# Output projection of a hybrid decoder layer in seven block products instead of eight, on one Trainium2 core

## The chip, the core and the metric

The kernel runs on one core of a Trainium2 chip. The metric is the time of one execution in device microseconds. TensorE (PE in the profile) multiplies, with its weight loads (PEld) beside it; VectorE (DVE) and ScalarE (ACT) work on tiles; GpSimd (POOL) does some element work and issues the accumulating DMAs; SyncE (SP) issues most DMAs.

## The reference

One decoder layer on 1024 tokens of width 1024. A normalised input goes through one in-projection to three groups of heads: four HGRN2 heads, a windowed attention mixture, and RWKV-7. Their outputs, side by side, are the rows that the output projection multiplies:

```
h <- h + W_out [ HGRN2(A) | dilated-window attention mixture(B) | RWKV-7(C) ](W_in rmsnorm(h))
h <- h + gated MLP with causal depthwise conv (width 3) on rmsnorm(h)
h <- h + sigmoid(rmsnorm(h) W_g) * (p[layer] W_p)
```

followed by a final RMSNorm. W_out is 1024 by 1024, so the output projection is a 1024 by 1024 by 1024 product. Everything is float32.

## The kernel before

Tokens lie along the free dimension, features over 128 partitions: a matrix of 1024 features is eight tiles of 128 by 1024, and most work is on token halves of 512 (HT). A float32 product is made of three TensorE products. Each factor is split into a rounded high part and the rest, and the sum takes high by high, high by low and low by high (`mm3`, the three matmul lines L142, L144, L146). A weight block of 128 output features is loaded by one DMA of 512 KB on SP (`load_w`, L105, two buffers `wraw`). `split2` makes its high part `whi` by a cast on ACT (L114) and its low part `wlo` either by a subtraction on DVE or POOL (L120), or by a negation on ACT (L117) and an accumulating DMA on GpSimd that adds the weights from DRAM to it (L118). There are six `whi` and six `wlo` buffers of half a block each.

The stages run in this order: norm of the input; in-projection, RWKV-7 (`rwkv`, head pairs 6 and 7), HGRN2 and window attention (tiles 0 to 3 and 4, 5), with the in-projection blocks of later heads fed between the steps of a head as filler for TensorE (`project_rest`); output projection (`phase_out`); the MLP, whose products are already made by a seven-product scheme (`mul`, L1343 and L1644); per-layer embedding; final norm.

Within an engine instructions run in the order in which they stand in its queue. A scheduler sets that order when the kernel is built, from a cost estimate of each instruction; `issue_after(x)` in the code holds back what is created under it until x stands in the order. The queues themselves are in order at run time, so an instruction that waits holds all behind it on its engine, and a waiting DMA issue on SP holds all later transfers of that queue.

Around RWKV-7, ACT makes `lora`, `sg` and `kksq` (squares of the keys), TensorE sums them (`kks`, L563), ACT makes the decay `w` (L573, L577), DVE its running product and inverse, ACT and DVE `r` (L506, L507), and TensorE the scores `sc` (L659). SP carries `sc` through DRAM (`scz`, `At`, L669, L675) to a DVE recurrence (`Tt`, `Tb`, L683, L685). At the end of the last HGRN2 head DVE updates the states `hst` (L1078), TensorE makes `hpo`, ACT and DVE normalise `ho` (L1091 to L1102), and TensorE transposes it (`vt`, L1108).

The output projection takes the eight head tiles as operands. `o_split` splits each as soon as its head is done, the low part of one token half on DVE, of the other on POOL. `phase_out` loads h (eight DMAs on ACT's queue), takes weight blocks in 14 turns (blocks 0 and 1 for both token halves, the others once for each half, so each is loaded twice), adds each product to h and stores it. The squares of the first half go to a sum (`sq_acc`), from which TensorE makes the norm factor (`ps_ss`, L188) while the second half is still being multiplied. It makes 8 blocks x 8 head tiles x 2 halves x 3 parts = 384 matmuls of 128x128 by 128x512.

## Time and profile before

| | |
|---|---|
| median of 3 runs | 1402.65 us (1402.52 to 1405.57) |
| the profiled execution | 1403.29 us, of which 1401.5 us are the span of its instructions |
| granted TensorE clock | 0.996 of full speed over the span |
| PE busy | 1373.6 us, 98% |
| DVE, ACT, POOL busy | 1042.6, 644.2, 361.7 us |
| the output phase | from 557 us (its first products, beside the last head) to 643 us (first product of the embedding) |

A row of the timeline reads: start, duration, engine, line, operation, out<-in, shapes, count, and in brackets the idle time before it and what ended that. In grouped rows the count is followed by busy time, mean ns of one, and idle time ahead of the group.

### The profile page before, as it was taken

The page shows a single profiled execution, that of the slowest core. Times are in us where ns is not written, and L with a number is a line of the kernel's source. Part 1 is how long each engine was busy: PE and PEld are TensorE (multiplying, and loading weights), DVE is VectorE, ACT ScalarE, POOL GpSimd, SP SyncE. Part 2 cuts the span into 40 slices and gives each one's busy share as a digit, 9 for nine tenths or more (in the row PEclk, how much of TensorE's full clock was granted, in tenths as well). Part 3 has the DMA queues.
Part 4 walks back from the last instruction along what each step waited for, and adds up shares of the span by engine and source line. Part 5 has one row for each costly group of instructions (what it writes and reads, how often), then busy time and mean ns, then how long its engine had stood idle before and what let it go on. Part 6 is the DMA issues. An engine that isn't in the chain of part 4 may idle for free.

```text
span 1401.5 us, 22421 instructions
## 1 busy us (share of the span) xinstructions
PE 1373.6 (98%) x8646; PEld 1114.8 (80%) x8646; DVE 1042.6 (74%) x1614; ACT 644.2 (46%) x1107; POOL 361.7 (26%) x286
## 2 busy tenths in 40 slices
PE   9999999999999999999999999999999999999997
PEld 6878777877878767788788888888888888888886
DVE  7595456835667795458889888888888799778675
ACT  7523323133355584365544343444344444455662
POOL 4210011101222232111345455445453000002231
PEclk9999999999999999999999999999999999999998
DMA  6344322533723322873232322232324963442674
GB/s 231 90 119 101 91 69 68 133 72 88 244 91 106 99 69 89 267 224 130 97 128 98 113 102 88 101 109 98 113 98 163 354 211 113 120 150 62 174 196 149
DMA packets 88475, 182.83 MB, mean 130 GB/s; under 512 B 20912, under 2 KB 23216, under 8 KB 88368
## 3 DMA queue, kind: packets, MB, share of 16 engines
q1 hardware_dynamic: 66784, 147.05, 31.0%
q0 software_dynamic: 9360, 18.88, 7.3%
q10 hardware_dynamic: 12224, 15.47, 3.2%
q8 instruction: 68, 1.11, 0.3%
q14 instruction: 39, 0.32, 0.1%
HBM read 134.96 MB, written 46.40 MB: 129 GB/s over the span
## 4 chain that ended last, share of the span: by engine, by line
PE 83%; issue 7%; DVE 5%; ACT 2%; POOL 2%; DMA 1%; SPq 0%; POOLq 0%; DVEq 0%; ACTq 0%
PE bg L1343 17%; PE bv L1343 13%; PE bv L1644 7%; PE bg L1644 7%; PE dp L142 6%; PE dp L146 6%; PE dp L144 6%; PE swq L1174 1%; PE bv L142 1%; PE bv L146 1%; PE bv L144 1%; PE hsc L1020 1%; PE zp L142 1%; PE bg L142 1%; PE bg L146 1%
## 5 line engine op out<-in xcount | busy, mean ns | idle before, releaser
L142 PE MATMUL dp<-xh,whi 128*128 128x512 f32 x544 | 187.1, 406 | 2.5 <-ACT xh L413 1.2
L144 PE MATMUL dp<-xl,whi 128*128 128x512 f32 x544 | 180.3, 393 | 0.6 <-DVE xl L414 0.5
L146 PE MATMUL dp<-xh,wlo 128*128 128x512 f32 x544 | 179.6, 392 | 0.5 <-DMA wlo<-in_w_out_dram 0.5
L120 POOL TENSOR_TENSOR wlo<-raw,whi 128x512 fp32r<-128x512 f32 x84 | 134.8, 1623 | 75.7 <-ACT whi L114 75.7
L114 ACT CAST whi<-wraw 128x512 fp32r<-128x512 f32 x120 | 72.9, 617 | 153.5 <-PE dp L144 115.4
L1343 PE MATMUL bg<-t,whi 128*128 128x512 f32 x352 | 133.4, 389 | 0.0
L144 PEld LDWEIGHTS dp<-xl,whi 128*128 128x128 f32 x544 | 102.3, 188 | 24.7 <-DVE xl L414 2.6
L146 PEld LDWEIGHTS dp<-xh,wlo 128*128 128x128 f32 x544 | 102.1, 188 | 24.7 <-issue 2.0
L142 PEld LDWEIGHTS dp<-xh,whi 128*128 128x128 f32 x544 | 98.9, 189 | 27.3 <-issue 5.9
L120 POOL TENSOR_TENSOR wlo<-s,whi 128x512 fp32r<-128x512 f32 x44 | 64.6, 1467 | 166.9 <-ACT whi L114 153.7
L1644 PE MATMUL bg<-t,whi 128*128 128x512 f32 x308 | 95.2, 390 | 0.0
L114 ACT CAST whi<-raw 128x512 fp32r<-128x512 f32 x88 | 52.5, 619 | 92.7 <-issue 48.6
L1644 PE MATMUL bv<-t,whi 128*128 128x512 f32 x308 | 94.8, 389 | 0.0
L114 ACT CAST whi<-s 128x512 fp32r<-128x512 f32 x66 | 38.9, 620 | 119.5 <-PE bg L1343 112.8
L1343 PEld LDWEIGHTS bg<-t,whi 128*128 128x128 f32 x352 | 66.0, 188 | 13.7
L118 POOL DMA_DIRECT2D wlo<-in_w_in_dram x28 | 24.8, 898 | 190.0 <-ACT wlo L117 161.6
L195 POOL TENSOR_TENSOR rst<-rst,mhalf 128x4 f32<-128x4 f32 (+1 forms) x9 | 10.1, 1127 | 233.7 <-DVE rst L191 218.0
L1640 ACT CAST t<-t 128x512 fp32r<-128x512 f32 x77 | 47.8, 622 | 45.4 <-PE bv L1644 31.1
L1343 PE MATMUL bg<-t,wlo 128*128 128x512 f32 x176 | 67.5, 389 | 0.0
L1644 PEld LDWEIGHTS bv<-t,whi 128*128 128x128 f32 x308 | 57.8, 188 | 12.0
L1644 PEld LDWEIGHTS bg<-t,whi 128*128 128x128 f32 x308 | 57.8, 188 | 11.9
L120 DVE TENSOR_TENSOR wlo<-wraw,whi 128x512 fp32r<-128x512 f32 x60 | 44.8, 751 | 29.4 <-ACT whi L114 16.5
(423 smaller groups left out, 3464.8 us busy)
## 6 DMA issues: line engine op xcount, KB each, us to landing
raw<-in_ffn_up_dram SPq DMA_DIRECT2D x44, 512.0 KB, 3.3
wraw<-in_w_in_dram SPq DMA_DIRECT2D x28, 512.0 KB, 3.8
z<-zst SPq DMA_DIRECT2D x18, 512.0 KB, 3.2
gb<-ct SPq DMA_DIRECT2D x33, 256.0 KB, 2.1
t<-gb SPq DMA_DIRECT2D x33, 256.0 KB, 2.8
t<-gt SPq DMA_DIRECT2D x33, 256.0 KB, 2.7
zl<-z SPq DMA_DIRECT2D x16, 512.0 KB, 4.6
wraw<-in_ple_gate_dram SPq DMA_DIRECT2D x16, 512.0 KB, 3.8
```

The source lines that it names most:

```text
L114: self.cast = nc.scalar.copy(hi, src).ins
L118: nc.gpsimd.dma_start(lo, eng, accum_op=ALU.add)
L120: eng.tensor_tensor(lo, src, hi.bitcast(F32), ALU.subtract)
L142: nc.tensor.matmul(ps[hf], wh, xh[hf], start=first, stop=False)
L144: nc.tensor.matmul(ps[hf], wh, xl[hf], start=False, stop=False)
L146: self.step = nc.tensor.matmul(ps[hf], wl, xh[hf], start=False, stop=last).ins
L195: nc.gpsimd.tensor_tensor(r2, r, self.mhalf[:, :n], ALU.pow)
L1020: nc.tensor.matmul(sc[g:g + 64, c, :], ks[:, c * P + g:c * P + g + 64], x, start=True, stop=True)
L1174: m = nc.tensor.matmul(pq[h][:, b:b + w], d["q"][hs, qb * P:nk], d["k"][hs, b:b + w], start=True, stop=True)
L1343: nc.tensor.matmul(ps, w[part == 2][:, s], X[k][part == 1], start=start and k == part == 0, stop=k == 3 and part == 2, skip_group_check=no ...
L1640: nc.scalar.copy(xh, x)
L1644: nc.tensor.matmul(ps[m], wt[part == 2][:, m * P:(m + 1) * P], (xh, xl)[part == 1], start=k == part == 0, stop=k == NK - 1 and part == 2)
```

## The change

The output projection is written as a 2 by 2 block product: W_out in four quarters (rows and columns of 512), the operand in four quarters (four heads by one token half each). Seven products of quarter size replace the eight. Each is four row blocks of 12 matmuls (four 128-rows by three parts), so 28 jobs and 336 matmuls.

- The products take sums and differences of quarters. Those of the operand are made by `o_done` and in `phase_out`: differences on DVE, negations on ACT, and eight accumulating DMAs on GpSimd within SBUF. Each sum is split into high and low by `pair`, always cast on ACT and subtracted on DVE (before, half of the 16 subtractions were POOL's).
- Four of the seven products take sums of quarters of W_out. `out_sums` makes these early, in steps that `project_rest` takes twice per in-projection block from the RWKV-7 stage on. For each of four row blocks it makes two loads of 256 KB on SP, three negations on ACT, five accumulating DMAs on GpSimd and four stores to DRAM on SP: 8 loads, 12 negations, 20 accumulating DMAs and 16 stores in all. Their two tiles have the buffers that `sq_acc` uses (`sqt`).
- All 28 jobs are held in one fixed order by `issue_after(self.ends[-1])`. Weights are loaded as 256 KB halves, five jobs ahead. The low parts of the first 10 are made on DVE, those of the other 18 by ACT and an accumulating DMA (before, 14 by the latter).
- The rows of W_out are put into the order of the heads on the host; the operand buffers of the first token half are two pools instead of one; the embedding's loads share the weights' two `wraw` buffers instead of two of their own.

The core of the diff:

```diff
+    def out_sums(self):
+        nc, wo = self.nc, self.a["w_out"]
+        self.S = [{n: self.zpool.tile([P, HT], F32, tag=f"ws{n}{i}", name=f"ws{n}{i}") for n in "1234"} for i in range(4)]
+        for i in range(4):
+            a11, a12, a21, a22 = (wo[m][:, c] for m in (i, 4 + i) for c in (slice(0, HT), slice(HT, T)))
+            t, u = (self.spool.tile([P, HT], F32, tag="sqt", name=self.nm("wsum"), bufs=2) for _ in (0, 1))
+            def turn(x):
+                nc.scalar.activation(x, x, AF.Copy, scale=-1.0)
+            def add(x, src):
+                nc.gpsimd.dma_start(x, src, accum_op=ALU.add)
+            nc.sync.dma_start(t, a21)
+            nc.sync.dma_start(u, a22)
+            yield
+            turn(t)
+            add(u, a21)
+            yield
+            nc.sync.dma_start(self.S[i]["1"], u)
+            add(t, a11)
+            yield
+            nc.sync.dma_start(self.S[i]["3"], t)
+            turn(u)
+            yield
+            turn(t)
+            add(u, a11)
+            yield
+            add(t, a22)
+            add(u, a12)
+            yield
+            nc.sync.dma_start(self.S[i]["2"], t)
+            nc.sync.dma_start(self.S[i]["4"], u)
+            yield
...
     def project_rest(self, js):
+                if k in (1, 5):
+                    next(self.sums, None)
...
+    FIRST, LAST = (6, 7, 0, 1), (4, 2, 3, 5)
+    def pair(self, dst, src, eng=None):
+        nc = self.nc
+        hi, lo = dst
+        nc.scalar.copy(hi, src)
+        (eng or nc.vector).tensor_tensor(lo, src, hi.bitcast(F32), ALU.subtract)
+    def o_done(self, k):
...
+        o = [self.o[k][:, HT:], self.o[k][:, :HT]]
+        if k in self.FIRST:
+            i = self.FIRST.index(k)
+            t1, t3 = self.Eo[i]
+            nc.vector.tensor_tensor(t1, o[1], o[0], ALU.subtract)
+            self.pair(self.A[i], o[0])
+            self.pair(self.B[i], t1)
+            nc.scalar.activation(t1, t1, AF.Copy, scale=-1.0)
+            nc.scalar.activation(t3, o[1], AF.Copy, scale=-1.0)
+            return
...
+        for t in self.Eo[i][::-1]:
+            nc.gpsimd.dma_start(t, self.parts[k, 1], accum_op=ALU.add)
     def phase_out(self, hp, x0, emb):
...
+        plan = {"p1": (A, "a", 0, 1), "p5": (B, "b", 4, 0), "p3": (D, "b", 0, 0), "p6": (A, "a", 0, 0),
+                "p7": (B, "a", 4, 0), "p2": (C, "c", 0, 1), "p4": (A, "a", 4, 1)}
+        jobs = [(n, i) for n in plan for i in range(4)]
...
+            with ExitStack() as order:
+                if self.ends:
+                    order.enter_context(self.tc.issue_after(self.ends[-1]))
+                self.mul((ps, ws.pop((n, i)), X, start))
+            self.ends.append(self.step)
...
+        for n, (p, i) in enumerate(jobs):
+            for q in range(0 if n == 0 else n + 4, min(n + 5, len(jobs))):
+                ws[jobs[q]] = weight(*jobs[q])
+            job(p, i)
+            for go in extra.get(n, ()):
+                go()
```

Where instructions move, at three places. First ACT in the RWKV-7 preparation. Before, from the first in-projection copy after the norm factor:

```order
L506 ACTIVATE lora_452<-raw_449,omm 128x1024
L502 COPY raw_456<-dp_160 128x1024
L114 CAST whi_654<-wraw_647 128x512
L506 ACTIVATE k_467<-dp_161,omm 128x1024
L514 ACTIVATE lora_452<-lora_452 64x1024
L506 ACTIVATE sg_459<-raw_456,omm 128x1024
L560 ACTIVATE kksq_477<-k_467,par 128x1024
L114 CAST whi_846<-wraw_844 128x512
```

and in the changed kernel, where `wsum` are the tiles of `out_sums`:

```order
L546 ACTIVATE lora_455<-raw_452,omm 128x1024
L542 COPY raw_459<-dp_163 128x1024
L114 CAST whi_677<-wraw_670 128x512
L546 ACTIVATE k_470<-dp_164,omm 128x1024
L554 ACTIVATE lora_455<-lora_455 64x1024
L440 ACTIVATE wsum_1118<-wsum_1118 128x512
L546 ACTIVATE sg_462<-raw_459,omm 128x1024
L600 ACTIVATE kksq_480<-k_470,par 128x1024
L114 CAST whi_873<-wraw_871 128x512
```

The first negation of the second row block's tile now stands between `lora` and `sg`.

Second SP's queue over the same stretch and after it. Before:

```order
L105 DMA wraw_518<-in_w_in_dram 128x1024
L105 DMA wraw_611<-in_w_in_dram 128x1024
L105 DMA wraw_647<-in_w_in_dram 128x1024
L105 DMA wraw_844<-in_w_in_dram 128x1024
L105 DMA wraw_920<-in_w_in_dram 128x1024
```

and in the changed kernel (`wsum_654`, `wsum_655` are the two tiles of the first row block, `wsum_1118`, `wsum_1119` of the second, `ws` the sums in DRAM):

```order
L105 DMA wraw_614<-in_w_in_dram 128x1024
L446 DMA wsum_655<-in_w_out_dram 128x512
L105 DMA wraw_670<-in_w_in_dram 128x1024
L451 DMA ws_638<-wsum_655 128x512
L105 DMA wraw_871<-in_w_in_dram 128x1024
L454 DMA ws_640<-wsum_654 128x512
L464 DMA ws_641<-wsum_655 128x512
L463 DMA ws_639<-wsum_654 128x512
L445 DMA wsum_1118<-in_w_out_dram 128x512
L446 DMA wsum_1119<-in_w_out_dram 128x512
L105 DMA wraw_947<-in_w_in_dram 128x1024
```

Loads and stores of the sums now stand between the weight loads; the load of `wsum_1118` comes behind the four stores of the first row block.

Third DVE at the end of the last HGRN2 head. Before:

```order
L1225 TENSOR_TENSOR ob_4988<-ob_4988,swd_5746 128x512
L1076 COPY hst_5760<-hkv_5761 128x128
L1078 SCALAR_TENSOR_TENSOR hst_5760<-hst_5760,hT_5207,hkv_5761 128x128 x3
L1078 SCALAR_TENSOR_TENSOR hst_5760<-hst_5760,hT_5207,hkv_5770 128x128 x3
L1097 TENSOR_REDUCE hss_5801<-hsq_5799 128x8
L1098 TENSOR_SCALAR hss_5801<-hss_5801 128x8
L1102 TENSOR_TENSOR ho_5777<-ho_5777,hrs_5804 128x1024
```

and in the changed kernel, from the fifth of the six updates on:

```order
L1118 SCALAR_TENSOR_TENSOR hst_5851<-hst_5851,hT_5290,hkv_5861 128x128
L1284 TENSOR_TENSOR t_1013_5967<-xh_5408,t_1012_5966 128x512
L1118 SCALAR_TENSOR_TENSOR hst_5851<-hst_5851,hT_5290,hkv_5861 128x128
L120 TENSOR_TENSOR wlo_6060<-wraw_6039,whi_6058 128x512
L1368 TENSOR_TENSOR xh_5406<-xh_5406,xh_5398 128x512
L1284 TENSOR_TENSOR t_1017_5971<-xh_5412,t_1016_5970 128x512
L1368 TENSOR_TENSOR xh_5408<-xh_5408,xh_5400 128x512
L1368 TENSOR_TENSOR xh_5412<-xh_5412,xh_5404 128x512
L1137 TENSOR_REDUCE hss_5892<-hsq_5890 128x8
L120 TENSOR_TENSOR wlo_6080<-wraw_6076,whi_6078 128x512
L1138 TENSOR_SCALAR hss_5892<-hss_5892 128x8
L1284 TENSOR_TENSOR xl_5383<-xh_5398,xh_5382 128x512
```

Splits of the operand sums (`t`, `xl`), the differences of operand tiles (`xh`) and a weight split stand between the state updates and between the steps of the norm.

More of the change, by code (lines that the diff above doesn't have):

```diff
@@ L1293, in phase_out @@
+        at(20, [factor, norm])
+        at(22, [lambda: [next(self.norm0, None) for _ in (0, 1)] for _ in range(6)])
+        self.ends = []
+        for n, (p, i) in enumerate(jobs):
[4 more added lines that the diff above has]
+                go()
+        for m in range(ND):
+            sums(m, 1)
+        ps, pb = small()
         self.ffn_first()
```

184 lines of the change are left out of this document (111 added, 73 removed).

## The prediction

> **What bounds the kernel now.** I read the page's busy shares and its chain of waits first, then the busy time by stage, then single instructions where the change meets the path.
>
> ```profile
> span 1401.5 us, 22421 instructions
> PE 1373.6 (98%) x8646; PEld 1114.8 (80%) x8646; DVE 1042.6 (74%) x1614; ACT 644.2 (46%) x1107; POOL 361.7 (26%) x286
> PE 83%; issue 7%; DVE 5%; ACT 2%; POOL 2%; DMA 1%; SPq 0%; POOLq 0%; DVEq 0%; ACTq 0%
> ```
>
> TensorE (PE) is busy for 98% of the span and makes 83% of the chain that ended last: matmuls taken away are time taken away, where nothing else is late. The stages that the change touches, busy time by window (columns: window, its length, then busy us of PE, weight loads, DVE, ACT, POOL):
>
> ```profile
> 30.00:75.00 45.00, 45.00 (x242) 36.80 (x241) 28.18 (x31) 25.94 (x37) 11.60 (x10) 1.00 0.36 88
> 580.00:600.00 20.00, 19.06 (x83) 15.16 (x83) 8.44 (x13) 9.43 (x16) 3.52 (x5) 1.00 0.87 223
> 600.00:645.00 45.00, 45.00 (x206) 37.37 (x205) 32.37 (x52) 26.86 (x48) 7.39 (x8) 1.00 0.62 177
> ```
>
> PE has no idle time from 30 to 75 us, where the first weight sums of the change will run, and loses 0.94 us in the first 20 us of the output phase. So the output phase is bound by its matmuls, and so is the early stage: a stall put into either is paid in full.
>
> **Part 1, the saving: 384 products become 336.** Two matmuls of the old output phase:
>
> ```profile
> 590.16 0.39 PE L144 MATMUL dp<-xl,whi 128*128 128x512 f32 x1
> 614.19 0.39 PE L146 MATMUL dp<-xh,wlo 128*128 128x512 f32 x1
> 590.10:614.20 24.10, 24.10 (x108) 1.00 0.84 216
> ```
>
> The window holds 108 matmuls, of which one had begun before it, so 106 steps lie between the two starts: (614.19 - 590.16) / 106 = 0.227 us each. Both kernels use the same 128x128 by 128x512 shape and the clock is granted at 1.00 here. 48 x 0.227 = **10.9 us less**.
>
> **Part 2, what the weight sums cost early on.** The sums are made from about 30 us on, between the in-projection blocks, by DMA alone: load a quarter of W_out, turn its sign on ScalarE (ACT), add other quarters with accumulating DMAs, store. They need no TensorE. But the ACT turns stand in ACT's own queue, ahead of work that TensorE waits for, and each waits for a transfer. Prices of the transfers, first the ten accumulating DMAs of the first 130 us (issue, landing), then a store and a load of the same 256 KB elsewhere in the kernel, then the issue at 36.0 us:
>
> ```profile
> L118 POOL DMA_DIRECT2D wlo<-in_w_in_dram x10: 857/878/1059, 26.2 to 117.9; - x10
> DMA to landing us min/median/max: 3.6/4.5/6.9
> gb<-ct SPq DMA_DIRECT2D x33, 256.0 KB, 2.1
> t<-gb SPq DMA_DIRECT2D x33, 256.0 KB, 2.8
> wlo<-in_w_in_dram POOLq DMA_DIRECT2D x1, 256.0 KB, 6.9
> ```
>
> Call the landing of an accumulating DMA L: between 3.6 and 6.9, and I take the median 4.5, because the sums spread over the same stretch as those ten. [...]
>
> The instructions that the turns meet, in the profile before:
>
> ```profile
> 29.91 23.86 SPq L105 DMA_DIRECT2D wraw<-in_w_in_dram  x4
> 50.31 1.14 ACT L506 ACTIVATE sg<-raw,omm 128x1024 f32<-128x1024 f32 x1
> 51.48 1.15 ACT L560 ACTIVATE kksq<-k,par 128x1024 f32<-128x1024 f32 x1
> 52.85 1.84 PE L563 MATMUL kks<-few,kksq 128*128 128x2 f32 x16
> 59.52 1.06 ACT L577 ACTIVATE w<-w 128x1024 f32<-128x1024 f32 x1
> 69.71 1.10 ACT L506 ACTIVATE r<-dp,omm 128x1024 f32<-128x1024 f32 x1
> 72.10 1.27 DVE L507 SCALAR_TENSOR_TENSOR r<-dp,par,r 128x1023 f32<-128x1023 f32 x1
> 77.23 1.52 PE L659 MATMUL sc<-ar,bhat 64*64 64x64 f32 x64 [0.82 <-DVE ar L614]
> 60.67 0.18 DVE L583 COPY dz<-w 128x16 f32<-128x16 f32 x1 [5.17 <-ACT w L577]
> ```
>
> First round. The load of the first block's second quarter (`wsum_655`) is queued on SP behind the weight load at 29.91, so it starts at 30.3 and lands, by 2.8 to 3.0 us, at 33.3. Then follow in a chain: its add (L), its store (2.1), a turn (0.6, as ACT's 128x512 casts take, 0.615 in the rows further down), two adds (2L), a store (2.1), the load of the next block's quarter into the same buffer (2.8), its turn (0.6). The end is 33.3 + 3L + 2.1 + 0.6 + 2.1 + 2.8 + 0.6 = 41.5 + 3L. That last turn (`wsum_1118`) stands just ahead of `sg` (50.31) and `kksq` on ACT. At L = 4.5 it ends at 55.0: **+4.7 us** on `kksq`. PE takes `kks` 0.2 us after `kksq` ends (51.48 + 1.15 = 52.63, PE at 52.85), with all later in-projection matmuls behind it, so PE stalls. Behind it also move the decay factors to `w` and all that DVE makes of it (DVE waits 5.17 us for `w`): a delay here is carried to `sc`.
>
> Second round. Behind `w` (59.52 + 1.06 = 60.6, plus the shift) come a turn (0.6), two adds (2L), the load of the third block (0.35 to issue, 2.8) and its turn (0.6), which stands ahead of `r` on ACT: 64.95 + 2L plus the shift, against `r` at 69.71 plus the shift. DVE takes `r` only at 72.10, 1.3 us after ACT has finished it, and in the new order half of the `kkn` pair goes first, another 0.7: 2.0 us of slack. The loss is 2L - 6.75, at L = 4.5 **+2.25 us**, and `sc` had no slack at all (0.82 us of waiting). Together 5L - 15.5 = **6.95 us**; 2.45 at L = 3.6, 16.4 at L = 6.4.
>
> Later rounds put four stores and a load ahead of `scz` and one ahead of `At` on SP, and adds ahead of `khat` on POOL. What they delay:
>
> ```profile
> 82.84 0.86 SPq L675 DMA_DIRECT2D At<-scz  x2
> 89.82 0.17 DVE L683 TENSOR_TENSOR Tt<-At,Tb 64x31 f32<-64x31 f32 x1
> 124.69 1.98 SPq L695 DMA_DIRECT2D Tc<-Tz  x4
> 133.03 1.20 PE L795 MATMUL py<-Tc,sc 32*32 32x32 f32 x64
> ```
>
> By the prices above `At` comes some 5 us later, beyond the shift that all shares. It was issued by 83.7; with about 4 us to land, the DVE recurrence `Tt` that reads it started some 2 us after it was there, and at its end `Tc`, issued by 126.7, was there some 3 us before PE took `py`. These 5 us cover it: I cost that at nothing, and at up to 3 us if they are less.
>
> **Part 3, the end of the last head.** PE's first products now stand ahead of `vt`, and DVE has five subtractions and a weight split between the six state updates:
>
> ```profile
> 549.32 2.33 DVE L1078 SCALAR_TENSOR_TENSOR hst<-hst,hT,hkv 128x128 f32<-128x128 f32 x6
> 506.58 1.75 DVE L120 TENSOR_TENSOR wlo<-wraw,whi 128x512 fp32r<-128x512 f32 x1
> 508.25 0.69 DVE L325 TENSOR_TENSOR zp<-zp,rstd 128x512 f32<-128x512 f32 x1
> 555.48 1.22 DVE L1097 TENSOR_REDUCE hss<-hsq 128x8 f32<-128x1024 f32 x1 [3.83 <-ACT hsq L1095]
> 560.03 1.07 PE L1108 MATMUL vt<-cst,ho 128*128 128x128 f32 x8 [1.80 <-DVE ho L1102]
> 510.10 0.66 PE L1054 MATMUL vt<-cst,hk 128*128 128x128 f32 x4 [2.42 <-ACT hV L1049]
> ```
>
> The updates finish later by five subtractions and a split, 6 x 0.69 = 4.1 us, less about 1.2 in which DVE waited for TensorE anyway, so `ho` comes 2.9 us later. Before the transposes PE now has 31 products instead of 23, 8 x 0.227 = 1.8 us of cover: +1.1. The wait of 2.42 us for `hV` should shrink by about 1.0, as POOL no longer makes operand subtractions there, beside which DVE's 128x512 subtraction took 1.75 us. Sum **+0.1**, ends -2 to +3.
>
> **Part 4, the output phase.** ACT in the old one, and PE's two waits:
>
> ```profile
> L114 ACT CAST whi<-wraw 128x512 fp32r<-128x512 f32 x19 | 11.5, 615 | 14.4 <-PE dp L144 10.3 <-PE dp L146 4.0
> L117 ACT ACTIVATE wlo<-whi 128x512 fp32r<-128x512 f32 x10 | 6.3, 631 | 0.3
> L220 ACT ACTIVATE sqt<-h 128x512 f32<-128x512 f32 x10 | 6.2, 629 | 3.9 <-DVE h L1263 3.4 <-issue 0.5
> 599.07 0.33 ACTq L1264 DMA_DIRECT2D hd<-h  x1
> 614.42 0.95 PE L188 MATMUL ps_ss<-few,acc 128*128 128x1 f32 x8
> PE dp L146 <- DMA wlo<-in_w_out_dram: 0.5, 1, 0.5
> PE dp L142 <- DVE h L1263: 0.4, 1, 0.4
> ```
>
> From the 13th to the 24th of the 28 jobs (12 x 12 x 0.227 = 32.6 us) ACT gets 12 casts of weights, 14 of operands and embeddings, 10 negations, 8 squares and 8 stores: 26 x 0.615 + 10 x 0.631 + 8 x 0.629 + 8 x 0.33 = 30 us. It is nearly full, and the last square, behind two weight casts and a pair of embedding casts, ends about 1.5 us after PE is ready for `ps_ss` (without a wait before): **+1.5**, ends 0 and 4. The 0.9 us that PE lost at 580 to 600 (waits for `h` and a weight) go, since job 13 has its weights well before: **-0.9**. The 8 accumulating operand DMAs are needed four jobs (10.9 us) after they start, against 6.9 at worst: nothing.
>
> **Sum.** -10.9 + 4.7 + 2.25 + 0.1 + 1.5 - 0.9 = -3.25. The profiled run took 1403.29 us (span 1401.5 and 1.8 around it), 0.64 above the median of 1402.65; from the median the forecast is **1399.4 us**.
>
> **Rivals.**
> 1. *The sums stay hidden.* No loss before 77 us; the rest gives -10.9 + 0.7 = -10.2, so 1392.4. For it: ACT is busy only 25.94 of 45 us from 30 to 75, and the saving is certain. Against it: 41.5 + 3L is under 50.31 only for L under 2.9, below all ten rows. [...]
> 2. *The first add is as slow as its neighbours were.* It runs beside two 512 KB loads, where the add at 36.0 took 6.9. With 6.9 for it and 4.5 for the rest the first round costs 7.1, the second 2.25: net -0.85, 1401.8, no change.
> 3. *Slower: the adds contend throughout.* The sums double the accumulating traffic here, and at L = 6.4 in both rounds ACT's two turns cost 16.4 us, more than the products save: -10.9 + 16.4 + 0.7 = +6.2, 1408.9. It decides from L = 5.1 on (5L - 15.5 = 10.2), and is over the bound from 5.9. For it: 6.9 in the row above. Against it: the median is 4.5, and DMA is 0.36 busy here.
> 4. *The output phase is bound by ACT or weights.* If each of the last dozen jobs waits 0.3 us, 4 us: 1402 to 1403. Against: the window shows PE fully busy at 0.62 DMA, and six weight buffers.
>
> **How the numbers follow.** Forecast 0.37 (1396 to 1402); rival 1 0.20 (1391 to 1395); rivals 2 and 4 together 0.27; rival 3 0.16. A measurement of this kernel tells about 0.3% (4.2 us) from no change: faster is under 1398.4, slower over 1406.9. Faster: rival 1 and two thirds of the forecast's own spread below 1399.4 and around L = 4.2, 0.20 + 0.24 = 0.44. Slower: nearly all of rival 3, 0.15. Same: the rest, 0.41. The range runs from L under 2.9 with a little gained at `vt` (1391) to L = 6.3 (1408).
>
> **What would show it.** Right, if ACT sits idle ahead of `wsum_1118`, released by a DMA, with `sg` near 55 us; PE waits for `kksq` some 4 to 5 us and for `ar` about 3; PE waits at `ps_ss` of the output phase; and the 28 jobs take 28 x 2.72 = 76.2 us plus that. Rival 1 shows PE with no wait at `kks`; rival 3 adds landing at 6 us or more and a wait at `kks` near 10. The forecast is wrong in its mechanism if PE's waits before 140 us are unchanged while the time is above 1396, for then the saving is lost at the tail or in the output phase.

## The result, and the profile after

The changed kernel takes 1444.4 us (median of four, 1442.46 to 1448.99) against 1403.6 us (four, 1402.52 to 1405.57): a ratio of 1.0294, with a 95% interval of 1.0266 to 1.0322. It is slower by 40.8 us; the forecast was 1399.4 us, and the range ended at 1408. The profiled execution took 1443.61 us.

The top of the page of the changed kernel:

```profile
span 1441.8 us, 22516 instructions
PE 1380.2 (96%) x8598; PEld 1114.9 (77%) x8598; DVE 1061.3 (74%) x1650; ACT 663.8 (46%) x1145; POOL 379.6 (26%) x310
```

PE has the 48 matmuls less that were counted (8598 against 8646) and is yet busy 6.6 us longer. Its idle time grew from 27.9 to 61.6 us (span less busy). So of the 40.3 us that the span grew, 33.7 are new idle time of PE, and the matmuls that are left cost 6.6 + 10.9 = 17.5 us more than before.

Where that happened is seen in two stretches: from 30 us to a point some 15 us ahead of the first `py` of RWKV-7 (which starts at 133.0 us before, 155.7 after), and from the first `hpo` of HGRN2 to the first product of the MLP. First before (columns: window, length, busy us of PE, weight loads, DVE, ACT, POOL, then granted clock, DMA share, GB/s):

```profile
30.00:118.00 88.00, 87.05 (x481) 70.66 (x480) 66.93 (x116) 38.09 (x54) 17.70 (x17) 1.00 0.39 105
437.70:666.20 228.50, 219.91 (x1645) 179.84 (x1644) 159.36 (x289) 123.96 (x227) 50.45 (x44) 1.00 0.47 147
```

and after:

```profile
30.00:140.00 110.00, 94.72 (x474) 74.29 (x473) 62.90 (x100) 43.73 (x66) 35.37 (x36) 0.91 0.75 176
459.30:706.40 247.10, 218.46 (x1598) 176.28 (x1597) 175.97 (x325) 138.11 (x254) 50.57 (x49) 0.95 0.52 149
```

The early stretch, with seven matmuls fewer, took 22 us longer: PE idle 15.3 us instead of 1.0, and busy 7.7 us longer. The late one took 18.6 us longer although 47 matmuls are gone from it: idle 28.6 instead of 8.6, and busy only 1.5 us less where 10.9 were saved. In both the granted clock is below 1. The rest of the span did not change: 319.7 us before and 319.3 after between the two stretches, and 735.3 and 735.4 us from the MLP's first product to the end.

PE's waits over the whole span of the changed kernel (engine, line, waited for: us in total, times, longest):

```profile
PE zo L1472 <- DVE h L1361: 9.0, 1, 9.0
PE dp L1472 <- DVE h L1361: 5.9, 5, 2.2
PE dp L142 <- DVE r L547: 5.5, 2, 4.7
PE ps_ss L203 <- POOL rst L197: 5.4, 1, 5.4
PE vt L1148 <- DVE ho L1142: 5.0, 2, 3.3
PE dp L142 <- DVE v L547: 3.6, 1, 3.6
PE dp L1472 <- ACT t L1490: 3.5, 1, 3.5
...
PE kks L603 <- ACT kksq L600: 1.6, 1, 1.6
```

**The clock.** PE's waits had a second price in this kernel. Windows of the changed kernel, the same columns:

```profile
48.00:54.00 6.00, 5.89 (x16) 4.83 (x17) 1.22 (x1) 3.13 (x5) 2.72 (x4) 0.50 0.77 113
...
616.00:624.00 8.00, 8.00 (x37) 6.63 (x36) 5.12 (x8) 6.15 (x11) 2.62 (x3) 1.00 0.75 160
```

The clock was granted at one half in nine stretches between 47.4 and 675.4 us, together 44.4 us, each 3.4, 6.8 or 10.2 us long. Before, there was none between 14 and 1392 us; the last 9 us of both kernels, where PE has almost no work, run at one half. In the first window 16 matmuls fill six microseconds; in the second, at full clock, 37 fill eight.

**The early stalls.** The timeline of the changed kernel, row by row from SP, ACT, POOL and PE:

```profile
38.92 0.33 SPq L451 DMA_DIRECT2D ws<-wsum  x1
44.31 0.63 ACT L440 ACTIVATE wsum<-wsum 128x512 f32<-128x512 f32 x1 [9.57 <-DMA ws<-wsum]
45.24 0.86 POOL L443 DMA_DIRECT2D wsum<-in_w_out_dram  x1 [6.84 <-ACT wsum L440]
...
46.70 1.36 POOL L197 TENSOR_TENSOR rst<-rst,mhalf 128x4 f32<-128x4 f32 x1
48.11 1.11 PE L203 MATMUL ps_ss<-cst,rst 128*128 128x128 f32 x4 [5.44 <-POOL rst L197]
...
59.74 0.63 ACT L440 ACTIVATE wsum<-wsum 128x512 f32<-128x512 f32 x1 [1.84 <-DMA wsum<-in_w_out_dram]
87.19 0.63 ACT L440 ACTIVATE wsum<-wsum 128x512 f32<-128x512 f32 x1 [6.16 <-DMA wsum<-in_w_out_dram]
87.72 1.10 ACT L546 ACTIVATE r<-dp,omm 128x1024 f32<-128x1024 f32 x1
129.05 0.63 ACT L440 ACTIVATE wsum<-wsum 128x512 f32<-128x512 f32 x1 [6.04 <-DMA ws<-wsum]
129.59 1.10 ACT L546 ACTIVATE v<-dp,omm 128x1024 f32<-128x1024 f32 x1
```

This is a chain over four queues. The second negation of the first row block (44.31) overwrites a tile whose store was issued at 38.92, so it waits 9.57 us for that store. The next add on POOL (45.24) waits for the negation, and behind it in POOL's queue stands `rst`, a step of the norm factor of the second token half (L197). PE waits 5.44 us for that factor at 48.11, with all of the in-projection behind it. The same happens again without POOL: negations that wait 6.16 and 6.04 us for transfers stand ahead of `r` and `v` on ACT.

**The late stalls.** The timeline of the changed kernel in the output phase, from PE, SP, ACT and DVE:

```profile
586.48 1.77 PE L1148 MATMUL vt<-cst,ho 128*128 128x128 f32 x8 [3.27 <-DVE ho L1142]
587.81 2.82 SPq L1481 DMA_DIRECT2D raw<-in_ffn_up_dram  x4
588.24 12.50 ACTq L1316 DMA_DIRECT2D h<-in_xT_dram  x8
596.03 0.69 DVE L1361 TENSOR_TENSOR h<-h,dp 128x512 f32<-128x512 f32 x1 [5.79 <-DMA h<-in_xT_dram]
...
609.13 1.19 PE L1472 MATMUL zo<-t,whi 128*128 128x512 f32 x2 [9.04 <-DVE h L1361]
```

The eight loads of h hold ACT's queue for 12.5 us, and four loads of the MLP's weights start beside them on SP. The product p3 goes into the accumulators of p5, so DVE must first have added p5 to h: the fixed order asks for all eight tiles of h within its first twelve jobs. The kernel before issued the same eight loads in less than half the time, and needed them one after the other:

```profile
562.21 5.72 ACTq L1246 DMA_DIRECT2D h<-in_xT_dram  x8
```

From 580 us on its additions to h are some 4 to 8 us apart, half a tile at a time.

### The profile page after: what moved, and what is told of

Its sections match the earlier page's. It is cut to its first block, busy times and chain, and to the rows that moved or that the text cites. A ratio compares the mean times of both kernels' runs of the same rounds, so it can differ in the third digit from the quotient of the medians.

```text
span 1441.8 us, 22516 instructions
## 1 busy us (share of the span) xinstructions
PE 1380.2 (96%) x8598; PEld 1114.9 (77%) x8598; DVE 1061.3 (74%) x1650; ACT 663.8 (46%) x1145; POOL 379.6 (26%) x310
## 4 chain that ended last, share of the span: by engine, by line
PE 77%; DMA 8%; DVE 6%; issue 4%; POOL 2%; ACT 2%; SPq 1%; POOLq 0%; ACTq 0%; DVEq 0%
PE bg L1472 16%; PE bv L1472 12%; PE bv L1774 7%; PE bg L1774 7%; PE dp L142 5%; PE dp L146 4%; PE dp L144 4%; DMA wsum<-in_w_out_dram 3%; DMA h<-in_xT_dram 2%; PE dp L1472 1%; PE bv L142 1%; PE bv L146 1%; PE bv L144 1%; PE swq L1214 1%; PE bg L142 1%
## 5 line engine op out<-in xcount | busy, mean ns | idle before, releaser
L142 PE MATMUL dp<-xh,whi 128*128 128x512 f32 x416 | 141.0, 415 | 9.5 <-DVE r L547 5.5
L144 PE MATMUL dp<-xl,whi 128*128 128x512 f32 x416 | 134.3, 399 | 0.8 <-DVE xl L415 0.7
L146 PE MATMUL dp<-xh,wlo 128*128 128x512 f32 x416 | 134.1, 397 | 0.6 <-POOL wlo L120 0.6
L142 PEld LDWEIGHTS dp<-xh,whi 128*128 128x128 f32 x416 | 76.0, 192 | 30.4 <-issue 10.1
L146 PEld LDWEIGHTS dp<-xh,wlo 128*128 128x128 f32 x416 | 79.3, 191 | 20.8 <-issue 2.7
L144 PEld LDWEIGHTS dp<-xl,whi 128*128 128x128 f32 x416 | 79.6, 191 | 19.9 <-DVE xl L415 2.6
L197 POOL TENSOR_TENSOR rst<-rst,mhalf 128x4 f32<-128x4 f32 (+1 forms) x9 | 11.7, 1297 | 234.6 <-DVE rst L193 218.7
L1774 PEld LDWEIGHTS bg<-t,whi 128*128 128x128 f32 x308 | 57.8, 188 | 11.9
L118 POOL DMA_DIRECT2D wlo<-in_w_in_dram x28 | 28.4, 1026 | 145.2 <-ACT wlo L117 120.2
L1771 DVE TENSOR_TENSOR t<-t,t 128x512 fp32r<-128x512 f32 x77 | 55.0, 715 | 7.8 <-ACT t L1770 7.6
```

The costliest lines, as they stand in the source:

```text
L118: nc.gpsimd.dma_start(lo, eng, accum_op=ALU.add)
L142: nc.tensor.matmul(ps[hf], wh, xh[hf], start=first, stop=False)
L144: nc.tensor.matmul(ps[hf], wh, xl[hf], start=False, stop=False)
L146: self.step = nc.tensor.matmul(ps[hf], wl, xh[hf], start=False, stop=last).ins
L197: nc.gpsimd.tensor_tensor(r2, r, self.mhalf[:, :n], ALU.pow)
L1771: V.tensor_tensor(xl, x, xh.bitcast(F32), ALU.subtract)
```

## The experiments

Each experiment was timed once, beside the kernel before (1402.25 us for the first four below, 1403.46, 1403.77 and 1406.43 for the next three groups of four). So the table gives places in the profile too, which tell where a difference arose: the start of the first `hpo`, that of the MLP's first product, and the stretch between the two, in us. "Before" and "after" are the two profiled kernels, with their median times. How far the last column can be trusted is seen in the six kernels that have the same new output phase, after, 3, 4, 5, 9 and 14: it lies between 245.3 and 251.3. A few microseconds there between single runs are not told apart; what a trace shows beyond that is which wait came or went.

| kernel | time | first `hpo` | MLP | between |
|---|---|---|---|---|
| before | 1403.6 | 437.7 | 666.2 | 228.5 |
| after | 1444.4 | 459.3 | 706.4 | 247.1 |
| 1 no sums | 1420.66 | 437.6 | 684.0 | 246.4 |
| 2 sums alone | 1427.82 | 461.3 | 690.8 | 229.5 |
| 3 filled wait | 1456.73 | 469.7 | 719.1 | 249.4 |
| 4 sums from block 5 | 1435.76 | 446.9 | 698.2 | 251.3 |
| 5 sums held from block 1 | 1439.53 | 452.5 | 702.3 | 249.8 |
| 6 MLP's loads later | 1442.68 | 448.6 | 705.1 | 256.5 |
| 7 h in halves | 1430.31 | 448.7 | 692.8 | 244.1 |
| 8 both | 1426.27 | 446.4 | 688.7 | 242.3 |
| 9 sums from block 12 | 1460.4 | 477.8 | 723.1 | 245.3 |
| 10 embedding later | 1457.94 | 477.6 | 720.1 | 242.5 |
| 11 head's end first | 1458.77 | 477.8 | 719.4 | 241.6 |
| 12 h on two queues | 1456.07 | 478.0 | 717.7 | 239.7 |
| 13 pairs apart | 1441.52 | 459.8 | 703.9 | 244.1 |
| 14 one step a block | 1443.7 | 457.1 | 706.5 | 249.4 |
| 15 all edits | 1431.98 | 456.0 | 692.5 | 236.5 |
| 16 all, no sums | 1413.82 | 436.5 | 675.1 | 238.6 |

### 1 and 2: the two halves of the change apart

Experiment 1 keeps the new output phase and makes no sums; the four products take plain quarters of W_out, so its output leaves the sums out.

```diff
-                if k in (1, 5):
-                    next(self.sums, None)
...
-   **{f"p{p}": lambda i, n=n: self.S[i][n] for p, n in ("51", "62", "73", "34")}}
+   **{f"p{p}": lambda i, m=m, c=c: wo[m + i][:, c] for p, m, c in
+      ((5, 0, left), (6, 4, left), (7, 0, right), (3, 4, right))}}
```

> The changed kernel without the weight sums: nothing of their loads, negations, adding DMAs and stores is made, and the products that take sums read plain quarters of W_out instead (so the output leaves the sums out). Theory Q (the sums' instructions stand in ACT's, POOL's and SP's queues and hold what TensorE waits for, and TensorE then runs at half clock for a while): all that was lost before the first HGRN2 products comes back. First hpo at 437 to 440 us (before 437.7, changed 459.3), no half clock between 30 and 150 us, time 1419 to 1425. Rival P (the prediction's own: only the turns ahead of kksq and r cost, 7 us): hpo near 452, time about 1437. What lies between hpo and the MLP stays: about 18 us more than before in either case.

Experiment 2 is the kernel before with the sums made and not used.

```diff
+                if k in (1, 5):
+                    next(self.sums, None)
```

> The kernel before with the weight sums alone added, stored and used by nothing; its output projection stays as it was. Theory Q: the sums alone cost about 20 us (1419 to 1428), PE waits for the norm factor rst near 48 us for 4 to 6 us, and clock 0.5 shows in three to five places before 150 us. Rival P: 7 us, 1408 to 1412. Rival R (the loss belongs to the new output projection, and the sums are hidden): 1403.

Measured: 1420.66 and 1427.82 us, 18.4 and 25.6 above the kernel before. The two places in each, of experiment 1:

```profile
L1125 PE MATMUL hpo<-hV,hS x64: 270/275/377, 437.6 to 556.0; 128*128 128x128 f32 x64
L1469 PE MATMUL bg<-t,whi x352: 389/389/389, 684.0 to 1095.5; 128*128 128x512 f32 x176
```

of experiment 2:

```profile
L1127 PE MATMUL hpo<-hV,hS x64: 270/275/377, 461.3 to 577.7; 128*128 128x128 f32 x64
L1382 PE MATMUL bg<-t,whi x352: 389/389/389, 690.8 to 1102.3; 128*128 128x512 f32 x176
```

Without sums the first `hpo` is where it was before (437.6 against 437.7), and the late stretch has its whole 17.9 us of loss. With sums alone the late stretch is as before (229.5 against 228.5), and the early loss is 23.6 us. The two losses are separate and nearly add up to the whole (18.4 + 25.6 = 44.0, against 40.8). PE's early waits of experiment 2 are those of the changed kernel:

```profile
PE dp L142 <- DVE r L546: 6.0, 2, 5.2
PE ps_ss L201 <- POOL rst L195: 5.4, 1, 5.4
PE dp L142 <- DVE v L546: 3.4, 1, 3.4
```

### 3: does the idle time halve the clock?

PE gets 22 matmuls that nobody needs, to fill the wait of 5.4 us; all else is the changed kernel.

```diff
+                for _ in range(22 * hf):
+                    nc.tensor.matmul(pb, X[0][0][0][:, :P], X[0][0][0], start=True, stop=True)
                 nc.scalar.copy(self.R[:, halves[hf]], self.rstd_spread(r, pb))
```

> The changed kernel with 22 more matmuls (128x128 by 128x512, result overwritten) put ahead of the second norm-factor spread, where PE waits 5.4 us. If an idle TensorE is what brings the half clock: the wait is filled (22 x 0.227 = 5.0 us), no half clock from 48 to 55 us, and kks stands 2 to 3.4 us earlier than in the changed kernel (62.5 us), although work was added. If the half clock has another cause (for example the DMA load): clock 0.5 at 48 to 55 as before, kks at 62.5 or later.

From the timeline of experiment 3, the filling, the next matmuls and a negation on ACT:

```profile
43.29 5.15 PE L408 MATMUL ps_ss<-xh 128*128 128x512 f32 x22
49.06 0.65 PE L203 MATMUL ps_ss<-cst,rst 128*128 128x128 f32 x4 [0.62 <-POOL rst L197]
50.00 0.63 PE L144 MATMUL dp<-xl,whi 128*128 128x512 f32 x2
...
62.17 0.63 ACT L442 ACTIVATE wsum<-wsum 128x512 f32<-128x512 f32 x1 [11.84 <-DMA wsum<-in_w_out_dram]
```

and its window of 48 to 54 us (busy us of PE, clock, DMA share, GB/s):

```profile
48.00:54.00 6.00, 5.38 (x26) 1.00 0.81 125
```

With PE kept at work the clock stays at 1.00 where it was 0.50, and a pair of matmuls takes 0.63 us where it took 1.05. Idle time brought the half clock there; the transfers beside it were much the same (DMA share 0.81 against 0.77). The time was no better, 1456.73 us: the scheduler, with PE's queue longer, put the next negation ahead of `lora`, it waited 11.84 us for its load, and PE waited 12.7 us at `kks`, with 17.1 us of half clock from 61 us on. The expectation on the clock held, that on the time fell, for a place in ACT's order that the edit had moved.

### 4, 5, 9 and 14: can the sums be put where they cost nothing?

The steps are held at the place where they are created, each on its own queue, behind the last weight cast, weight load and accumulating weight add; the scheduler can no longer draw them ahead. Experiment 5 does that with the steps as they were, two per in-projection block; experiment 4 starts only at the fifth block. A block is 48 matmuls, 48 x 0.227 = 10.9 us of PE's work, so two steps a block are one per 5.5 us of that work. In time they are further apart, since a block alternates with the steps of a head: the steps of experiment 5 run from 30 to 299 us.

```diff
-                if k in (1, 5):
-                    next(self.sums, None)
+                if k in (1, 5) and self.blk > 4:      # experiment 5: > 0
+                    with self.tc.issue_after(self.cast), self.tc.issue_after(self.wdma), self.tc.issue_after(self.wadd):
+                        next(self.sums, None)
```

> The changed kernel with the sums begun at the fifth in-projection block of the filler instead of the first, and each of their steps held on its engine behind that block's weight DMA, cast and adding DMA, so that they cannot run ahead. Theory Q: no PE wait over 2 us before 80 us, early loss 22 us down to 0 to 8 (first hpo at 438 to 446), time 1421 to 1431. Rival P: hpo near 452, time about 1437. If the sums cost by DMA traffic wherever they stand, hpo stays near 459.

> The changed kernel with the sums begun at the first filler block as before, but each step held on ACT, SP and POOL behind that block's weight cast, weight DMA and adding DMA. Separates place from order. If it is the running ahead of the steps (the scheduler puts a turn where its transfer has not landed) that costs: hpo at 438 to 448 us, time 1425 to 1435, no worse than with the late start (1435.8, hpo 446.9), since the steps are over before the second RWKV pair's recurrence, where that run waited 4.2 and 2.7 us. If it is the place in the first pair's preparation: PE waits over 3 us before 90 us, hpo 450 to 459.

Measured: the early loss fell from 21.6 to 9.2 us (4) and 14.8 us (5), with the first `py` where it was before, at 132.7 us in both (133.0). What is left comes later, at the second head pair. Of experiment 5:

```profile
302.68 0.31 PE L838 MATMUL py<-Tc,sc 32*32 32x32 f32 x2 [4.55 <-DMA Tc<-Tz]
```

A store of a sum in SP's queue waits for its add, and `Tc` waits behind it. So between about a third and more than half of the early loss was the place that the scheduler had chosen for the steps, and holding them does not remove the rest. In experiment 4 PE's longest wait there is another, 4.2 us at `yt` for DVE.

Experiment 9 makes the sums from the twelfth block on, three steps per block and one per half block; in its trace the first load is issued at 224.1 us, the first negation runs at 263.6 and the last store is issued at 439.9. (The expectation puts that block at about 290 us.) Experiment 14 makes them throughout, one step per block with few exceptions, and the rest in the half blocks at the end.

```diff
+                if k in (1, 3, 6) and self.blk > 11:                   # experiment 9
+                if k == 1 or (k == 5 and self.blk in (9, 18)):         # experiment 14
...
+                next(self.sums, None)        # both: per half block of project_late, held likewise
```

> The changed kernel with the sums begun only at the twelfth filler block (about 290 us, where DMA is busy for 0.07 to 0.5 of the time and no recurrence of RWKV waits for SP), three held steps per block and one per half block of the late in-projection; the output phase as changed. Theory Q (it is what the sums stand in front of, not their work, that costs): hpo at 437 to 441 us, no half clock between 30 and 450 us, time 1418 to 1425, as without the sums (1420.7). Rival: they cost by their DMA traffic and issue slots wherever they are, 8 to 15 us, time 1428 to 1436.

> The changed kernel with one held step of the sums per in-projection block (10.9 us apart; 20 steps, then one per late half block) from the first block on. Theory Q' (a step placed less than one landing after the one before it makes its in-order queue wait; the loss falls with the distance): 22.7 us at the scheduler's own pace, 9 to 15 at 5.5 us, 0 to 5 here: hpo at 437 to 443, time 1420 to 1427. Rival (traffic, slots, or SP's stores ahead of the RWKV transfers at any pace): hpo at 446 to 455, time 1430 to 1440.

Measured: first `hpo` at 477.8 and 457.1 us. In experiment 9 the loss is 40 us, the largest of all placements. In experiment 14 hardly anything is lost as long as there is one step per block: the last `py` of the second pair is at 292.6 against 290.7. Then come the half blocks. Of experiment 14:

```profile
421.16 0.63 ACT L440 ACTIVATE wsum<-wsum 128x512 f32<-128x512 f32 x1 [6.15 <-DMA ws<-wsum]
...
423.12 1.12 PE L1065 MATMUL hsc<-qt,ks 128*64 128x64 f32 x16 [11.06 <-ACT ks L1052]
```

The distance between two steps explains this: each step needs the transfer of the one before it, and where the next step comes up sooner than that, the queue that holds it stands still and passes the wait on (in the rows above ACT stood still for 6.15 us, and PE for 11.06). Experiments 5 and 14 begin at the same block and differ in that distance: up to the last `py` of the second pair two steps per block cost 14.4 us (305.1 against 290.7) and one per block 1.9. Experiment 9 fits, but its steps stand in other places too, so what its 40 us owe to the distance alone is not shown. A version with one step per block all along would have to begin earlier or use other tiles; it was not tried.

### 6, 7 and 8: the loads of h

All three stand on experiment 4. Experiment 6 holds the MLP's first weight loads behind the twentieth weight half of the output phase. Experiment 7 loads h in 16 halves in the order in which the jobs need them. Experiment 8 does both.

```diff
-        self.ffn_first()
+        with self.tc.issue_after(wd[19]):
+            self.ffn_first()
...
-            nc.scalar.dma_start(self.h[k], self.a["xT"][k])
+        for k, c in [*((4 + i, 0) for i in range(4)), *((i, 1) for i in range(4)),
+                     *((i, 0) for i in range(4)), *((4 + i, 1) for i in range(4))]:
+            nc.scalar.dma_start(self.h[k][:, c * HT:(c + 1) * HT], self.a["xT"][k][:, c * HT:(c + 1) * HT])
```

> The run with the late sums, and the first four 512 KB loads of the MLP's weights held on SP behind the weight load of the 20th job, where before they went out at 587.8 us beside the eight h loads. Theory S (the long wait for h is the DMA traffic of 6 MB at once): the 9.7 us wait falls to 2 to 5, the half clock after it to 3 to 7 us, time 1424 to 1430. Rival T (the order of the h loads on ACT's queue sets it, whatever runs beside): wait 8 to 10, time 1434 to 1437. If the MLP then waits for its weights, that shows at its first product.

> The run with the late sums, and h loaded as sixteen halves of 256 KB in the order in which the products are added to them, instead of eight whole tiles; the MLP loads stay where they were. Rival T: the 9.7 us wait falls to 0 to 4, because only half of the 4 MB is wanted before the first accumulating job. Theory S: falls by half at most, 4 to 8.

> Both edits together on the run with the late sums. If S and T each hold a part: the wait at zo is under 2 us, the half clock of the output phase under 8 us in all (24 to 27 before), time 1418 to 1426. If the time stays over 1430, another resource (DVE's queue, the embedding's loads in the shared weight buffers) takes the place of the wait.

Measured, against the 251.3 us of experiment 4 for the late stretch: 256.5, 244.1 and 242.3. The later loads halved the wait of `zo` for h (9.7 to 5.2 us), and PE's waits of `dp` for h went from 6.2 to 10.9. The halves took away the wait of `zo` for h, and 5.4 us of it came back as a wait of `zo` for ACT, which still issued h. What the later loads cost, in experiment 8:

```profile
606.52 0.69 DVE L1589 TENSOR_TENSOR s<-raw,raw 128x512 f32<-128x512 f32 x1 [4.15 <-DMA raw<-in_ffn_up_dram]
...
607.86 0.80 PE L1478 MATMUL dp<-xh,whi 128*128 128x512 f32 x1 [3.97 <-DVE h L1366]
```

DVE's sum of MLP weights now waits for its late load, in front of the addition to h that PE needs. So the loads of h made the wait at `zo`, and halves in the order of need take it away. What that is worth is less sure: the late stretch is 7.2 us shorter than in experiment 4, but 1.2 us shorter than in the shortest of the six kernels with the same phase. Whether the later loads of the MLP add anything to it (1.8 us) is not told apart.

### 10, 11 and 12: three more waits of the output phase

On experiment 9 with the MLP's loads behind the 24th half and h in halves, experiment 10 moves the embedding's loads, which share the weights' buffers, from job 16 to job 22; 11 also puts four splits of operand sums behind the end of the last head on DVE; 12 also puts half of h's loads on POOL's queue. Experiment 10 makes three edits to experiment 9 at once, so it does not price the embedding's loads alone.

```diff
-        at(16, [pools, *(lambda a=a: self.pe_load(*a()) for a in
+        at(16, [pools])
+        at(22, [*(lambda a=a: self.pe_load(*a()) for a in
...
-        at(3, [lambda i=i: self.pair(D[i], Lo[i][1]) for i in range(4)])
+            with self.tc.issue_after(self.vtail):
+                self.pair(D[i], Lo[i][1])
...
-            nc.scalar.dma_start(self.h[k][:, c * HT:(c + 1) * HT], ...
+            (nc.gpsimd if c == (k >= 4) else nc.scalar).dma_start(self.h[k][:, c * HT:(c + 1) * HT], ...
```

> The run with the sums from 290 us, with h in sixteen halves in order of need, the MLP's first weights held behind the 24th job's weight load, and the four embedding loads and their casts put from job 17 to 20 to jobs 23 to 26, behind the last weights of the shared buffers. Theory S+T (h traffic) and U (the embedding loads hold the two weight buffers, and their casts stand on ACT and DVE ahead of casts and sums that TensorE waits for): waits of dp for h 9.3 down to under 3 us, half clock in the output phase under 7 us in all, time 1404 to 1414. Rival: the embedding, which follows the last job, now waits for its operands, 3 to 8 us, and the gain of U is given back: 1412 to 1420.

> As the run before it, with the first split of the operand sums (D) held on DVE and ACT behind the last head's final product, so that it no longer stands between the head's state updates and norm. If those splits make the wait of 3.3 us at vt: the wait falls to 1 to 2 us and the half clock after it goes, 2 to 4 us less than the run before it. If the splits are then late for the third product, a wait of zo for t takes its place.

> As the run before it, with the eight h halves that are wanted last issued on POOL's queue instead of ACT's. If ACT is held by issuing h (it issued the eight loads over 12.5 us in the changed kernel): ACT is free 5 to 10 us earlier, its weight casts are in time, and the time is 1 to 4 us less than the run before it; if not, the same within 1.5 us.

Measured: the late stretch took 242.5, 241.6 and 239.7 us, the last 5.6 below experiment 9; the single steps are too small to be told apart. The long wait of `zo` for h is gone in all three. The wait at `vt` went from 3.3 to 1.7 us in 11, as before the change, but `zo` then waited 3.1 us for the splits that had been put back.

### 13: two jobs in one accumulator tile

Five waits of `dp` for DVE's addition to h recur every other job. Neighbouring jobs share one accumulator tile; if the second half of the tile is given to PE only when DVE has read the first, that makes these waits. Experiment 13 is the changed kernel with the four row blocks in the order 0, 2, 1, 3.

```diff
-        jobs = [(n, i) for n in plan for i in range(4)]
+        jobs = [(n, i) for n in plan for i in (0, 2, 1, 3)]
```

> The changed kernel with the four row blocks of each product run in the order 0, 2, 1, 3, so that the two halves of one PSUM tile are no longer written by jobs next to each other. In the changed kernel PE waits five times, 5.9 us in all, before the second job of such a pair, for DVE's add of the first (dp waits for h). Theory V (a tile's second half is held until the add of the first has read it): these waits go, 5 to 6 us less, 1437 to 1440. Rival: DVE's add is late in its own queue, and the waits only move one job on: 1442 to 1446.

Its waits from 560 to 720 us:

```profile
PE zo L1472 <- DVE h L1361: 9.0, 1, 9.0
PE ps_ss L190 <- DVE acc L223: 4.5, 2, 3.8
...
```

All five are gone (5.9 us), so the shared tile made them. With them went the 3.5 us that the list of the changed kernel gives to `t`, a cast of h for the MLP that this product does not read: DVE's addition to h of the job before, in the same tile, ended beside that cast (670.44 + 0.68, PE at 671.27). The late stretch is only 3.0 us shorter, and 3.8 us came up at the norm factor. The time, 1441.52 us, is 3 us from the median of the changed kernel, whose own four times spread over 6.5 us.

### 15 and 16: all edits together

Experiment 15 has the edits of 10 to 14 together; experiment 16 the same without sums, as in experiment 1.

```diff
-                if k in (1, 5):
+                if k == 1 or (k == 5 and self.blk in (9, 18)):         # 15; 16 has no step at all
...
-        jobs = [(n, i) for n in plan for i in range(4)]
+        jobs = [(n, i) for n in plan for i in (0, 2, 1, 3)]
```

> All edits together: sums at one step per block, h in halves in order of need on two queues, the MLP's and the embedding's loads late, the tail's splits late, the pairs apart. By the segments measured so far (from the first hpo to the MLP 239.7 us with the edits but without the pairs, 228.5 in the kernel before): 437 to 443 + 234 to 236 + 735 behind: 1407 to 1416. It beats the kernel before only if the segment falls under 228.

> The run with all edits, but without the sums (left out; the products that take sums read plain quarters of W_out). Tells the worth of the seven products when the sums are free: hpo at 437 to 439, the segment 232 to 237, time 1405 to 1411 by what was measured; 1395 if the remaining waits were all due to the sums.

Measured: 1431.98 and 1413.82 us, with a late stretch of 236.5 and 238.6 us. The edits are worth 12.9 us there beside experiment 14, and 7.8 beside experiment 1, both more than the six like phases differ. But even with the sums for nothing the seven-product phase is 10.1 us longer than the eight-product phase of before (238.6 against 228.5). What is left in experiment 16, from 540 to 690 us:

```profile
PE dp L1477 <- DVE h L1360: 5.7, 2, 4.6
PE zo L1477 <- DVE t L1281: 4.3, 1, 4.3
```

and 13.6 us at half clock. No version that was run reaches the kernel before: the closest, experiment 16, has no sums and is still 7.4 us above the kernel that was timed beside it.

## Why the prediction was wrong

**The saving (part 1) was right.** 48 matmuls are gone, and at full clock those that are left stand about 0.22 us apart (8.00 / 37). What failed is the sentence that matmuls taken away are time taken away "where nothing else is late": in both stretches something else was.

**The early sums (part 2): +6.95 forecast, 21.6 us measured, 23.6 alone.** The mechanism was named rightly, turns that wait for transfers in ACT's queue ahead of PE's work, but the step that listed the places was incomplete. It priced the negations ahead of `kksq` and `r`. Both are there (`sg` begins at 60.28 us, where 55 was to be the sign), with 1.6 us of PE's waiting where 4.7 were forecast and 4.7 where 2.25 were (PE stood at `dp`, whose accumulators `r` reads, not at `sc`, which waited 0.5). Three things were not in the sum:
- The first row block's own negation and the add behind it. The working followed the first row block only as a chain to `wsum_1118`, as if its own turn and its add stood ahead of nobody. They stood ahead of weight casts and, on POOL, of `rst`; this is the wait of 5.44 us, the largest of the early stretch. POOL's queue was looked at for `khat` alone. The store, too, was priced at 2.1 us; issued at 38.92, it let the negation begin at 44.31.
- The later rounds, costed "at nothing, and at up to 3 us". A negation ahead of `v` alone cost 3.6 us. The slack of 2 us at `At` was read from SP's two issues alone; ACT issues the other two, from 84.30 on.
- The clock, 7.7 us of the 22.

The price of the adds was not at fault. The 20 accumulating DMAs into the sums' tiles (L443) landed in the changed kernel after (minimum, median, maximum):

```profile
DMA to landing us min/median/max: 3.7/4.7/6.6
```

The median is near the 4.5 that was taken, and with 4.7 the working's own formula, 5L - 15.5, gives 8.0 us. So rival 3, which had all adds at 6.4 us and the loss from that, is not what happened, though its sign was. (By that formula rival 3 passes the bound from 6.0 on, not from 5.9.) Rival 1, hidden sums, falls with experiment 2.

**The end of the last head (part 3): +0.1 forecast, 0.9 measured** (1.5 more at `vt`, 3.3 against 1.8, where 1.1 was forecast, and 0.6 less at `hV`, 1.8 against 2.4, where 1.0 was), within its ends; the stretch at half clock that begins there was not in it.

**The output phase (part 4): +0.6 forecast, without the saving, and between 28 and 29 us measured** (18.6 longer although 10.9 were saved, less the 0.9 of part 3), the clock's price included. The step that failed is the last one, "the 0.9 us that PE lost at 580 to 600 (waits for `h` and a weight) go". It looked at the weight only. The diff puts p3 into the accumulators of p5, and so asks for the whole of h by the twelfth job; from that followed the 9.0 us at `zo`. Experiment 7 shows that the loads of h made that wait, and experiment 13 that the shared accumulator tiles made the waits of `dp`, 5.9 and 3.5 us. The wait at `ps_ss`, forecast at 1.5, was 0.7. Rival 4 had the right side, a phase bound by something other than matmuls, but named ACT and weights and gave it 4 us; from 560 to 720 us PE has no wait for a weight in its list, and h is what it waited for. ACT did stand still, for 11.9 us, while it issued h.

**The range** took in no case in which the order of the queues costs more than the matmuls save, apart from slow adds. A row that pointed to it was there: 5.17 us of DVE waiting for `w` showed that work already stood behind ACT.

**What stays open.** The sums at one step per block throughout, how much of the late loss each wait is worth, and the last 10 us of the late stretch. Another order of the seven products, which needs h later, was not tried.

## What to carry to other kernels

Work that needs no busy engine is not free where its steps stand in queues that run in order (here the sums alone cost 23.6 us): list every queue that each step enters, with what stands behind it there, and give two steps that depend on each other's transfers more distance than a transfer takes (here one step per 10.9 us of PE's work cost 1.9 us and two 14.4). A product order that saves matmuls by reusing accumulators also changes when every other operand is needed (here PE waited 9.0 us for h); list these times, loads off the path too, before counting the saving. And price a stall of TensorE above its own length where the profile shows its clock falling too: here nine waits of 1.58 to 9.04 us came with 44.4 us at half clock.

## What the runs showed of the hardware

In the changed kernel TensorE's granted clock fell to one half nine times between 47.4 and 675.4 us, for 3.4, 6.8 or 10.2 us each time. Each fall came during one of PE's waits or at most 1.94 us after its end; in order, these waits took 5.44, 1.58, 4.69, 3.57, 1.77, 3.27, 9.04, 2.17 and 3.45 us. Beside 33.7 us of new idle time the matmuls that are left took 17.5 us longer. Not only the long waits are among the nine. The one of 2.17 us in the timeline of the changed kernel, and the windows ahead of the fall and behind it (columns: window, length, PE busy, clock, DMA share, GB/s):

```profile
647.74 0.47 PE L1472 MATMUL dp<-xh,whi 128*128 128x512 f32 x1 [2.17 <-DVE h L1361]
...
644.69:648.10 3.41, 1.24 (x6) 1.00 1.11 275
648.10:651.51 3.41, 3.41 (x10) 0.50 0.93 232
```

In the kernel before, a wait of 2.42 us at `vt` (the row at 510.10) had no such effect:

```profile
508.41:511.82 3.41, 1.72 (x28) 1.00 0.63 225
511.82:515.24 3.42, 3.42 (x28) 1.00 0.48 83
```

The windows here and below have borders 3.41 us apart, laid so that the changes of the clock in the same trace fall on them (in the changed kernel the fall at 648.12 us, in the kernel before the changes at 13.45 and 1392.43). In the changed kernel PE was busy for 0.00, 1.94, 0.66, 0.65, 1.64, 0.20, 0.00, 1.24 and 0.74 us of the window ahead of each of the nine falls; and for 1.67 us of the one from 555.97 to 559.38, with a wait of 1.74 us at `vt`, behind which the clock stayed at 1.00. So neither the length of a wait nor PE's share of such a window tells alone whether half clock follows; what does, these runs do not show.
